# Two-layer hybrid decoder on one core: another order of copies, squares, splits and transposes where a layer begins

## The chip, the cores and the metric

The kernel runs on one core of one Trainium2 chip. The metric is the device time of one execution in microseconds, the median of several runs; lower is better. The core has five engines that work side by side, each through its own queue in order: PE (matrix products), ACT (ScalarE), DVE (VectorE), POOL (GpSimd) and SP, which here only issues DMAs. An engine waits at the head of its queue until what the instruction needs is there; nothing behind it can overtake.

## What is computed

Two layers act on x (256 rows, 2048 columns, float32). Cut to what matters here:

```python
for l in range(2):
    h = rms_norm(x, norm_pre[l])              # x * rsqrt(mean(x*x)) * g
    proj = h @ w_in[l]                        # q, k, v, gates, S5 and pool inputs
    att = nsa_mixer(...)                      # sparse attention
    ssm = s5_mixer(...)                       # state-space layer
    pool = pool_mixer(...)
    out = concat(att, ssm, pool) @ w_out[l]
    x = x + rms_norm(out, norm_post[l])
```

## The kernel before

**Products in three passes.** Each float32 operand is split into a high and a low part. ACT writes the high part (`split`, L311, a copy), DVE the low part (L317, the difference), and `mm3` (L387, L388, L389) adds high·high, high·low and low·high. So every block of weights needs one ACT and one DVE instruction before PE can use it. Weights come as a stream of pieces; a piece has two halves of 128x1024, which SP loads into five `raw` buffers in order (`load`, L285).

**Where a layer begins.** x is used transposed (`hT`, high and low). `turn(l, t, x, hT, c)` makes four of its 128x128 blocks: t is the row block (0 or 1), c a chunk of 512 columns (0 to 3). PE transposes (L411), ACT writes the high parts (L415), DVE the low ones (L421). The first product of a layer is `vs`: `vsel(n, t, c)` multiplies chunk (t, c) with half c of the four `vs` halves, 12 matmuls each, and sums over c in one PSUM bank per t. The normalisation is by the row, so the factor `rr` is multiplied in afterwards: the squares of x are summed (`square_sum`, ACT, L938; in the first layer some on DVE, L978), `rstd_of` takes the power of -0.5 on POOL (L397), `vsel_out(t)` scales the finished `vs` bank out of PSUM (L381 on ACT, L382 on DVE), and `row_factors` spreads `rr` along the columns (L433 on DVE, L434 on PE, L436).

**PSUM banks.** The tag `pp` has three banks. The two `vs` sums hold two, the first of the `u5` products (48 matmuls each; here U0, U1, U2) takes the third. U1 needs the bank that `vsel_out(0)` frees, U2 that of `vsel_out(1)`.

**Where a layer ends.** `wo` sums the output projection over 16 steps for each of four column chunks. For the last chunk (`mm_last(t, d)`, 12 matmuls for each t and d) the order is written by hand together with the start of the next layer: `ev_wo` squares the sum (ACT) and multiplies it with the norm weights (DVE, L1227), `rstd_of` gives the factor (DVE L395, then POOL L397), `update` adds the result to x (DVE, L1234, four chunks), and `turn` follows.

**What sets the order.** Inside `with tc.manual_schedule(engines=ORDERED)` each engine's queue has the order of the code. Outside, a scheduler places the instructions at build time; these may also be put among those written by hand. Of the S5 layer, `s5_chain` clears two matrices (`sa`, `sb`) in which only blocks are written later. The 128x2048 tiles of tag `m8` have four places: three hold `vs` halves, later `sa`, `sb` and the mixed outputs lie there. At the end of a layer the four mixed outputs fill them, so the next layer's second `vs` half can only be split when `mm_last(1, 0)` has read the first mixed output.

Of the kernel before, what the change touches and what calls it, by code (L numbers as in the profile page):

```python
# [138 lines left out]
def body(ctx, tc, a):  # L139
# [35 lines left out]
    X = {}  # L175
# [278 lines left out]
    def s5_chain(l):  # L454
# [8 lines left out]
        with after("pool"):  # L463
            G.memset(sa[:, 1024:], 0.0)
            G.memset(sb[:, :1280], 0.0)
# [476 lines left out]
    hT = new_hT()  # L942
# [8 lines left out]
    with tc.manual_schedule(engines=ORDERED):  # L951
        warm = st([128, 256], "r1", bufs=2)
        V.memset(warm, 0.0)
        load_x0(0, 0, 512)
        nc.sync.dma_start(cn[:, :160], a["cst"][:, :160])
        load_x0(0, 1, 512)
        load(0, (0,))
        load_x0(0, 2, 512)
        load_x0(0, 3, 512)
# [3 lines left out]
        load(1)  # L963
        nc.sync.dma_start(cn[:, 160:], a["cst"][:, 160:])
        nc.sync.dma_start(sm, a["sm"])
        load(2)
        wp = pp()
        for _ in range(5):
            T.matmul(wp[:, :256], lhsT=warm[:, :128], rhs=warm, start=True, stop=True)

        def both(t, c):
            low = turn(0, t, xt[t], hT, c)
            low()
# [9 lines left out]

        both(0, 0)
        both(0, 1)
        split(0, 0)
        both(0, 2)
        both(0, 3)
        sq_a(0, 0)
        vsel(0, 0, 0)  # L990
        both(1, 0)
        both(1, 1)
        vsel(0, 1, 0)
        split(0, 1)
        sq_a(0, 1)
        vsel(0, 0, 1)
        vsel(0, 1, 1)
        both(1, 2)
        split(1, 0)
        both(1, 3)  # L1000
        vsel(0, 0, 2)
        vsel(0, 1, 2)
        split(1, 1)
        sq_a(0, 2)
        sq_a(0, 3)
        vsel(0, 0, 3)
        vsel(0, 1, 3)
        sq_v(1, 0)
        sq_v(1, 1)
        sq_a(1, 2)  # L1010
        sq_a(1, 3)
        for t in range(2):
            X["norm"] = rstd_of(sqs[t], dst=X["rr"][:, t:t + 1]) and X["norm"]
# [3 lines left out]
    while n < nst:  # L1017
# [49 lines left out]
        elif kind == "vs":  # L1067
            X["gates"] = st([128, 2, 24], "gates")
            load(n + 4)
            with after("norm"), after("act"):  # L1070
                for h in range(2):
                    split(n + 2, h)
                for t in range(2):
                    vsel_out(t)
                row_factors()
# [118 lines left out]
        else:  # L1194
# [28 lines left out]
            def ev_wo(t, c):  # L1223
                p = X["op"][t]
                cs = slice(c * 512, (c + 1) * 512)
                square_sum(p, X["osq"][t], c)
                V.tensor_tensor(X["og"][t][:, cs], p, X["gpost"][:, cs], op=ALU.mult)  # L1227

# [21 lines left out]
            elif q == 0:  # L1250
# [8 lines left out]
                if l + 1 == NL:  # L1259
                    for t in range(2):  # L1260
                        for d in range(4):
                            mm_last(t, d)
                        ev_wo(t, 3)
                        update(t, rstd_of(X["osq"][t]))
                else:
# [4 lines left out]
                    def squares(t):  # L1270
                        for c_ in range(4):
                            square_sum(X["xt"][t][:, c_ * 512:(c_ + 1) * 512], sqs[t], c_)
                        rstd_of(sqs[t], dst=rr[:, t:t + 1])

                    with tc.manual_schedule(engines=ORDERED):
# [3 lines left out]
                        ev_wo(0, 3)  # L1279
# [123 lines left out]
```

## Time and profile before

| what | value |
|---|---|
| median of 3 runs | 884.55 us (883.99 to 885.16) |
| the profiled execution's own time | 880.77 us |
| its span, first to last instruction | 879.0 us |
| PE busy | 857.0 us of the span (97%) |
| DVE, ACT, POOL busy | 649.9, 487.9, 34.9 us |
| mean granted PE clock | 0.993 of full speed |

The profile is of one execution. PE is almost never idle, so the question is where in the span its 22 us without work lie: the page's tenths and the table by stretches show the first 30 us, some of 440 to 470 us (the border between the layers) and the last 9 us. Times in the rows count from the start of the span. "Idle before" and the name behind the arrow say how long an engine stood before an instruction and what ended that.

### The profile page before, as it was taken

What the parts mean: (1) busy time and instruction counts of PE and PEld (TensorE: products, weight loads), DVE (VectorE), ACT (ScalarE), POOL (GpSimd) and SP (SyncE); (2) the same over time, 40 slices, a digit from 0 to 9 for tenths busy, and PEclk for the clock granted to TensorE, in tenths of its full rate; (3) what the DMA queues carried; (4) which work ended last, traced back from release to release, by engine and by line L of the source; (5) the groups of instructions that cost most, each with busy time, mean ns of one, the idle gap of its engine ahead of it and who ended that gap; (6) DMA issues with size and microseconds to landing.
All of it is one profiled execution on the core that took longest, in us unless ns stands there. A gap on an engine that the chain in (4) does not pass through costs nothing.

```text
span 879.0 us, 17460 instructions
## 1 busy us (share of the span) xinstructions
PE 857.0 (97%) x6858; PEld 793.4 (90%) x6858; DVE 649.9 (74%) x1365; ACT 487.9 (56%) x961; POOL 34.9 (4%) x64
## 2 busy tenths in 40 slices
PE   7899999999999999999998999999999999999996
PEld 5898899999999999888898988999999999998884
DVE  4997889796887877557588676979778788765553
ACT  5755557584767743446375525475647666434440
POOL 0240000000000000000001300000000000000000
PEclk9999999999999999999998999999999999999998
DMA  8777656443445755557355577664444457456642
GB/s 296 243 211 264 244 194 203 139 146 121 147 141 164 250 196 170 192 191 265 142 195 191 167 290 262 194 200 120 146 129 160 128 184 264 149 187 191 191 145 97
DMA packets 46259, 165.04 MB, mean 188 GB/s; under 512 B 5536, under 2 KB 5792, under 8 KB 45152
## 3 DMA queue, kind: packets, MB, share of 16 engines
q1 hardware_dynamic: 43632, 154.22, 53.4%
q0 software_dynamic: 2544, 9.70, 3.1%
q8 instruction: 54, 0.88, 0.4%
q14 instruction: 29, 0.24, 0.1%
HBM read 158.66 MB, written 4.19 MB: 185 GB/s over the span
## 4 chain that ended last, share of the span: by engine, by line
PE 93%; DVE 2%; issue 2%; ACT 1%; DMA 1%; POOL 0%; DVEq 0%; POOLq 0%; ACTq 0%
PE pp L387 24%; PE pp L389 23%; PE pp L388 23%; PE acc L389 3%; PE acc L387 3%; PE acc L388 3%; PE acc L1113 2%; PE sc L592 2%; PE tr L749 1%; PE acc L597 1%; DVE hT L421 1%; PE tr L568 1%; PE acc L620 1%; DMA raw<-in_w 1%; PE sc L389 1%
## 5 line engine op out<-in xcount | busy, mean ns | idle before, releaser
L311 ACT ACTIVATE whi<-raw 128x1024 fp32r<-128x1024 f32 (+2 forms) x238 | 248.7, 1048 | 241.0 <-PE pp L388 103.0
L387 PE MATMUL pp<-hT,whi 128*128 128x256 f32 x1280 | 367.8, 287 | 2.2 <-DVE rs L403 2.0
L317 DVE TENSOR_TENSOR wlo<-raw,whi 128x1024 fp32r<-128x1024 f32 (+2 forms) x238 | 287.0, 1208 | 109.4 <-ACT whi L311 107.3
L388 PE MATMUL pp<-hT,whi 128*128 128x256 f32 x1280 | 365.1, 285 | 0.0
L389 PE MATMUL pp<-hT,wlo 128*128 128x256 f32 x1280 | 364.9, 285 | 0.0
L387 PEld LDWEIGHTS pp<-hT,whi 128*128 128x128 f32 x1280 | 246.0, 192 | 8.3 <-issue 4.9
L389 PEld LDWEIGHTS pp<-hT,wlo 128*128 128x128 f32 x1280 | 246.1, 192 | 3.2 <-issue 1.2
L388 PEld LDWEIGHTS pp<-hT,whi 128*128 128x128 f32 x1280 | 246.2, 192 | 1.4 <-issue 0.6
L388 PE MATMUL acc<-wlo,m 128*128 128x512 f32 x112 | 44.0, 393 | 0.0
L387 PE MATMUL acc<-whi,m 128*128 128x512 f32 x112 | 43.7, 390 | 0.0
L387 PE MATMUL pp<-whi,m 128*128 128x512 f32 x112 | 43.6, 390 | 0.0
L388 PE MATMUL pp<-wlo,m 128*128 128x512 f32 x112 | 43.6, 389 | 0.0
L389 PE MATMUL pp<-whi,m 128*128 128x512 f32 x112 | 43.6, 389 | 0.0
L389 PE MATMUL acc<-whi,m 128*128 128x512 f32 x112 | 43.6, 389 | 0.0
L512 ACT ACTIVATE m<-m 64x256 f32<-64x256 f32 x64 | 26.4, 413 | 11.8 <-DVE m L510 11.1
L378 ACT ACTIVATE a<-tr 128x256 fp32r<-128x256 f32 (+1 forms) x32 | 15.6, 488 | 24.9 <-PE tr L749 24.5
L734 ACT ACTIVATE P<-sc,sv 128x128 f32<-128x128 f32 (+1 forms) x64 | 26.1, 414 | 5.9 <-DVE scv L795 3.5
L742 ACT ACTIVATE P<-P,sv 128x128 f32<-128x128 f32 (+1 forms) x64 | 25.5, 448 | 2.0 <-DVE sv L740 1.0
L389 PEld LDWEIGHTS pp<-whi,m 128*128 128x128 f32 x112 | 21.0, 188 | 4.4
L389 PEld LDWEIGHTS acc<-whi,m 128*128 128x128 f32 x112 | 21.0, 188 | 4.4
L388 PEld LDWEIGHTS acc<-wlo,m 128*128 128x128 f32 x112 | 21.0, 188 | 4.3
L388 PEld LDWEIGHTS pp<-wlo,m 128*128 128x128 f32 x112 | 21.0, 188 | 4.3
(300 smaller groups left out, 1355.9 us busy)
## 6 DMA issues: line engine op xcount, KB each, us to landing
raw<-in_w SPq DMA_DIRECT2D x272, 512.0 KB, 3.6
raw<-in_w SPq DMA_DIRECT2D x8, 420.0 KB, 4.6
a<-in_gpost POOLq DMA_DIRECT2D x2, 1024.0 KB, 4.9
a<-in_x POOLq DMA_DIRECT2D x2, 1024.0 KB, 6.6
xs<-a SPq DMA_DIRECT2D x2, 1024.0 KB, 3.8
a<-xs POOLq DMA_DIRECT2D x2, 1024.0 KB, 7.5
out_dram<-a SPq DMA_DIRECT2D x8, 256.0 KB, 2.5
raw<-in_w SPq DMA_DIRECT2D x4, 280.0 KB, 3.1
```

The source lines that it names most:

```text
L311: A.activation(hi[:, :w], raw[:, :w], AF.Copy)
L317: V.tensor_tensor(lo[:, :w], raw[:, :w], hi[:, :w].bitcast(F32), op=ALU.subtract)
L378: A.activation(hi, src, AF.Copy)
L387: T.matmul(out, lhsT=lh, rhs=rh, start=start, stop=False, **kw)
L388: T.matmul(out, lhsT=lh, rhs=rl, start=False, stop=False, **kw)
L389: T.matmul(out, lhsT=ll, rhs=rh, start=False, stop=stop, **kw)
L421: X["norm"] = V.scalar_tensor_tensor(hT[1][:, k, ts], p[:, j * 128:(j + 1) * 128], C["gT"][:, l * 16 + k:l * 16 + k + 1], hT[0][:, k, ts]. ...
L512: A.activation(dst[64 * g:64 * g + 64, :, k0:k0 + 4, 16 * g:16 * g + 16], x[64 * g:64 * g + 64], AF.Copy)
L592: T.matmul(xv[:, i, m_, :], lhsT=IN[:, i, m_, :], rhs=u4[:, i, t, :], start=True, stop=True)
L734: A.activation(P[:, b], pv[:, b], AF.Exp, scale=-1.0, bias=sv[:, 0, b:b + 1], accum_out=sv[:, 1, b:b + 1])
L742: A.activation(P[:, b], P[:, b], AF.Copy, scale=sv[:, 2, b:b + 1])
L1113: T.matmul(hm[32 * j:32 * j + 32, :256], lhsT=blk[:, lk, :], rhs=raw[:, j * 256:j * 256 + 256], start=lk < 4, stop=lk >= 28, tile_position ...
```

## The change

The order of the instructions where each layer begins is written anew; two matrices are cleared on another engine; one warm-up matmul is added.

- At the first layer's start SP loads the first `vs` half before x, and the transposes, copies, splits, products and squares are interleaved in another way. The squares of the first row block stand together on ACT ahead of the others' end, `rstd_of` for that block follows at once, and `vsel_out(0)` and the splits of U0 move into the part written by hand.
- At the border of the layers `ev_wo` runs `rstd_of` ahead of the multiplication with the norm weights; the first row block's squares come before its transposes, the second's between its transposes; both splits of a piece come earlier; `vsel_out(0)` and the splits of U0 are written by hand ahead of the last two `vs` products.
- In the last layer `ev_wo` gets the same order of `rstd_of` and multiplication.
- `sa` and `sb` are cleared by ACT (a copy with scale 0) instead of two POOL memsets.

```diff
-        with after("pool"):
-            G.memset(sa[:, 1024:], 0.0)
-            G.memset(sb[:, :1280], 0.0)
+        for z in (sa[:, 1024:], sb[:, :1280]):
+            A.activation(z, bc(ident[:, 0:1], [128, z.shape[1]]), AF.Copy, scale=0.0)
...
-        load_x0(0, 0, 512)
+        load(0, (0,))
         nc.sync.dma_start(cn[:, :160], a["cst"][:, :160])
-        load_x0(0, 1, 512)
-        load(0, (0,))
-        load_x0(0, 2, 512)
-        load_x0(0, 3, 512)
+        for c in range(4):
+            load_x0(0, c, 512)
         load_x0(1, 0, 1024)
         load(0, (1,))
         load_x0(1, 1, 1024)
         load(1)
+        load(2, (0,))
         nc.sync.dma_start(cn[:, 160:], a["cst"][:, 160:])
         nc.sync.dma_start(sm, a["sm"])
-        load(2)
+        load(2, (1,))
         wp = pp()
-        for _ in range(5):
+        for _ in range(6):
...
+        split(0, 0)
         both(0, 0)
         both(0, 1)
-        split(0, 0)
         both(0, 2)
+        both(1, 0)
+        vsel(0, 0, 0)
+        split(0, 1)
         both(0, 3)
-        sq_a(0, 0)
-        vsel(0, 0, 0)
-        both(1, 0)
         both(1, 1)
         vsel(0, 1, 0)
-        split(0, 1)
-        sq_a(0, 1)
         vsel(0, 0, 1)
+        split(1, 0)
+        both(1, 2)
         vsel(0, 1, 1)
-        both(1, 2)
-        split(1, 0)
+        vsel(0, 0, 2)
+        split(1, 1)
         both(1, 3)
-        vsel(0, 0, 2)
         vsel(0, 1, 2)
-        split(1, 1)
-        sq_a(0, 2)
-        sq_a(0, 3)
         vsel(0, 0, 3)
-        vsel(0, 1, 3)
+        split(2, 0)
+        for c in range(4):
+            sq_a(0, c)
+        rstd_of(sqs[0], dst=X["rr"][:, 0:1])
         sq_v(1, 0)
         sq_v(1, 1)
+        split(2, 1)
         sq_a(1, 2)
         sq_a(1, 3)
-        for t in range(2):
-            X["norm"] = rstd_of(sqs[t], dst=X["rr"][:, t:t + 1]) and X["norm"]
+        vsel_out(0)
+        vsel(0, 1, 3)
+        rstd_of(sqs[1], dst=X["rr"][:, 1:2])
...
-            def ev_wo(t, c):
+            def ev_wo(t, c, first=None):
                 p = X["op"][t]
                 cs = slice(c * 512, (c + 1) * 512)
                 square_sum(p, X["osq"][t], c)
+                r = None if first is None else rstd_of(X["osq"][t], first)
                 V.tensor_tensor(X["og"][t][:, cs], p, X["gpost"][:, cs], op=ALU.mult)
+                return r
...
-                        ev_wo(t, 3)
-                        update(t, rstd_of(X["osq"][t]))
+                        update(t, ev_wo(t, 3, rstd_first(X["osq"][t])))
...
                         first = rstd_first(X["osq"][0])
-                        ev_wo(0, 3)
+                        r = ev_wo(0, 3, first)
                         mm_last(1, 0)
                         mm_last(1, 1)
                         hT = new_hT()
-                        r = rstd_of(X["osq"][0], first)
-                        split(m, 0)
                         update(0, r, False)
                         keep(0)
+                        split(m, 0)
+                        split(m, 1)
+                        for c_ in range(4):
+                            sq_a(0, c_)
                         for c_ in range(4):
                             turn(l + 1, 0, X["xt"][0], hT, c_)()
                         X["hT"] = hT
-                        split(m, 1)
                         mm_last(1, 2)
                         split(m + 1, 0)
+                        split(m + 1, 1)
                         mm_last(1, 3)
                         first = rstd_first(X["osq"][1])
-                        ev_wo(1, 3)
-                        r = rstd_of(X["osq"][1], first)
-                        split(m + 1, 1)
+                        r = ev_wo(1, 3, first)
                         update(1, r, False)
                         keep(1)
...
+                            if c_ == 1:
+                                rstd_of(sqs[0], dst=rr[:, 0:1])
+                            if c_ == 2:
+                                split(m + 2, 0)
+                            sq_a(1, c_)
+                        vsel_out(0)
+                        split(m + 2, 1)
                         vsel(m, 1, 2)
                         vsel(m, 1, 3)
-                        squares(1)
+                        rstd_of(sqs[1], dst=rr[:, 1:2])
```

**Place 1: ACT at the first layer's start.** Before, the queue begins as below. `tr`, `sc`, `acc` are the banks of the transposes of chunks 0, 1, 2 and, with `sc` again, 3; `a_1` and `a_2` are the two row blocks of x; `m_18`, `m_27`, `m_30` are `vs` halves 0, 1, 2.

```order
L415 ACTIVATE hT_84<-tr_120,cn 128x128 x4
L415 ACTIVATE hT_84<-sc_133,cn 128x128 x4
L311 ACTIVATE m_18_146<-raw_96 128x1024
L415 ACTIVATE hT_84<-acc_149,cn 128x128 x4
L415 ACTIVATE hT_84<-sc_162,cn 128x128 x4
L938 ACTIVATE mr_175,sq_86<-a_1_82 128x512
L415 ACTIVATE hT_84<-tr_192,cn 128x128 x4
L415 ACTIVATE hT_84<-sc_205,cn 128x128 x4
L311 ACTIVATE m_27_230<-raw_101 128x1024
L938 ACTIVATE mr_233,sq_86<-a_1_82 128x512
L1156 ACTIVATE hb_3848<-sm 128x8
L415 ACTIVATE hT_84<-acc_259,cn 128x128 x4
```

Now the same queue, with halves 0, 1, 2 in `m_16`, `m_24`, `m_27`:

```order
L311 ACTIVATE m_16_121<-raw_93 128x1024
L415 ACTIVATE hT_84<-tr_124,cn 128x128 x4
L415 ACTIVATE hT_84<-sc_137,cn 128x128 x4
L415 ACTIVATE hT_84<-acc_150,cn 128x128 x4
L415 ACTIVATE hT_84<-tr_163,cn 128x128 x4
L311 ACTIVATE m_24_191<-raw_101 128x1024
L415 ACTIVATE hT_84<-sc_194,cn 128x128 x4
L415 ACTIVATE hT_84<-sc_207,cn 128x128 x4
L311 ACTIVATE m_27_244<-raw_104 128x1024
L464 ACTIVATE m_66_500<-cn 128x1024
L464 ACTIVATE m_67_501<-cn 128x1280
L415 ACTIVATE hT_84<-acc_247,cn 128x128 x4
```

The split of half 0 moved to the front, chunk (1, 0) ahead of (0, 3), half 2 ahead of chunk (1, 2); the squares moved behind these rows, and the two clearings (L464) stand ahead of chunk (1, 2).

**Place 2: DVE at the border of the layers.** Before, from the low parts of the first row block's last chunk to the low parts of the second's first chunk. `acc_5119` is the bank of `mm_last(1, ...)`, `a_660` the second row block of x.

```order
L421 SCALAR_TENSOR_TENSOR hT_5236<-sc_5286,cn,hT_5235 128x128 x4
L317 TENSOR_TENSOR m_771_5299<-raw_5122,m_771_5299 128x1024
L317 TENSOR_TENSOR m_772_5314<-raw_5128,m_772_5314 128x1024
L402 TENSOR_REDUCE rs_5329<-sq_4659 128x1
L403 TENSOR_SCALAR rs_5329<-rs_5329 128x1
L1227 TENSOR_TENSOR a_655_4654<-acc_5119,a_656_4655 128x512
L395 SCALAR_TENSOR_TENSOR rs_5329<-sq_4659,rs_5329 128x1
L317 TENSOR_TENSOR wlo_5338<-raw_5130,whi_5337 128x1024
L1234 SCALAR_TENSOR_TENSOR a_660_4662<-a_655_4654,rs_5329,a_660_4662 128x512 x4
L421 SCALAR_TENSOR_TENSOR hT_5236<-tr_5373,cn,hT_5235 128x128 x4
```

Now the same stretch, where the bank is `acc_5120`:

```order
L421 SCALAR_TENSOR_TENSOR hT_5239<-sc_5298,cn,hT_5238 128x128 x4
L317 TENSOR_TENSOR m_776_5323<-raw_5129,m_776_5323 128x1024
L484 TENSOR_TENSOR m_816_5596<-rot 128x512
L544 TENSOR_TENSOR m_816_5596<-spv,cn 128x256
L317 TENSOR_TENSOR wlo_5327<-raw_5131,whi_5326 128x1024
L402 TENSOR_REDUCE rs_5342<-sq_4660 128x1
L403 TENSOR_SCALAR rs_5342<-rs_5342 128x1
L395 SCALAR_TENSOR_TENSOR rs_5342<-sq_4660,rs_5342 128x1
L1223 TENSOR_TENSOR a_655_4655<-acc_5120,a_656_4656 128x512
L1231 SCALAR_TENSOR_TENSOR a_660_4663<-a_655_4655,rs_5342,a_660_4663 128x512 x4
L421 SCALAR_TENSOR_TENSOR hT_5239<-tr_5382,cn,hT_5238 128x128 x4
```

The last step of the row factor (L395) moved ahead of the multiplication, the split of the fourth `vs` half ahead of both, and two S5 instructions (L484, L544) came in between; half 1 is split earlier, ahead of these rows.

**Place 3: ACT behind the second row block's last transposes.** Before, from these transposes' copy to the scaling of the first `vs` bank (L381). `sq_5152` and `sq_5153` take the squares of the two row blocks.

```order
L415 ACTIVATE hT_5235<-sc_5448,cn 128x128 x4
L938 ACTIVATE mr_5473,sq_5152<-a_659_4660 128x512
L311 ACTIVATE whi_5533<-raw_5140 128x1024
L311 ACTIVATE whi_5537<-raw_5142 128x1024
L311 ACTIVATE whi_5566<-raw_5524 128x1024
L938 ACTIVATE mr_5475,sq_5152<-a_659_4660 128x512
L311 ACTIVATE whi_5601<-raw_5526 128x1024
L311 ACTIVATE whi_5638<-raw_5529 128x1024
L938 ACTIVATE mr_5510,sq_5153<-a_660_4662 128x512
L311 ACTIVATE whi_5668<-raw_5531 128x1024
L381 ACTIVATE a_777_5346<-pp_5347,rr_5154 128x256
```

(Of the eight squares three stand here; the others lie between the same rows.) Now, from the clearing of `sa` on:

```order
L464 ACTIVATE m_815_5595<-cn 128x1024
L937 ACTIVATE mr_5345,sq_4660<-acc_5120 128x512
L464 ACTIVATE m_816_5596<-cn 128x1280
L415 ACTIVATE hT_5238<-tr_5382,cn 128x128 x4
L937 ACTIVATE mr_5407,sq_5154<-a_660_4663 128x512
L415 ACTIVATE hT_5238<-sc_5409,cn 128x128 x4
L415 ACTIVATE hT_5238<-acc_5441,cn 128x128 x4
L311 ACTIVATE whi_5466<-raw_5141 128x1024
L415 ACTIVATE hT_5238<-sc_5472,cn 128x128 x4
L937 ACTIVATE mr_5497,sq_5154<-a_660_4663 128x512
L381 ACTIVATE a_781_5355<-pp_5356,rr_5155 128x256
```

The scaling of the first bank moved from behind six splits and eight squares to the place right behind the last transposes' copy and its square.

## Rows read from the trace of the kernel before

**Rows 1.** The page, busy time of each engine.

```profile
PE 857.0 (97%) x6858; PEld 793.4 (90%) x6858; DVE 649.9 (74%) x1365; ACT 487.9 (56%) x961; POOL 34.9 (4%) x64
```

**Rows 2.** Stretches: length, busy time and instructions of each engine, PE clock, DMA share, GB/s.

```profile
50.00:60.00 10.00, 10.00 (x86) 10.00 (x85) 10.00 (x23) 5.41 (x8) 3.95 (x7) 1.00 0.61 197
...
466.00:468.00 2.00, 2.00 (x11) 2.00 (x11) 2.00 (x2) 0.10 (x1) 2.00 (x3) 0.50 0.72 203
```

**Rows 3.** Timeline of PE at the start: start, length, instruction.

```profile
24.68 0.39 PE L388 MATMUL pp<-m,hT 128*128 128x256 f32 x1 [0.96 <-DVE m L317]
...
36.30 0.36 PE L387 MATMUL pp<-hT,whi 128*128 128x256 f32 x1
```

**Rows 4.** SP's timeline, and DMA issues of 3.3 to 3.8 us with median time to landing.

```profile
3.07 1.21 SPq L949 DMA_DIRECT2D a<-in_x  x2
...
a<-in_x SPq DMA_DIRECT2D x1, 512.0 KB, 7.2
```

**Rows 5.** Timeline of ACT in the first 31 us.

```profile
8.62 1.11 ACT L311 ACTIVATE m<-raw 128x1024 fp32r<-128x1024 f32 x1
9.57 1.19 ACT L415 ACTIVATE hT<-acc,cn 128x128 fp32r<-128x128 f32 x4
10.56 1.23 ACT L415 ACTIVATE hT<-sc,cn 128x128 fp32r<-128x128 f32 x4
...
29.35 0.63 ACT L938 ACTIVATE mr<-a 128x512 f32<-128x512 f32 x1
...
30.10 0.63 ACT L938 ACTIVATE mr<-a 128x512 f32<-128x512 f32 x1
```

**Rows 6.** Costliest groups of the page, the S5 copy: busy and mean ns.

```profile
L512 ACT ACTIVATE m<-m 64x256 f32<-64x256 f32 x64 | 26.4, 413 | 11.8 <-DVE m L510 11.1
```

**Rows 7.** Timelines of ACT, DVE, POOL and PE at the border, 429 to 446 us.

```profile
434.04 1.14 ACT L415 ACTIVATE hT<-tr,cn 128x128 fp32r<-128x128 f32 x4 [4.19 <-PE tr L411]
...
439.37 2.35 DVE L317 TENSOR_TENSOR m<-raw,m 128x1024 fp32r<-128x1024 f32 x2
...
442.48 0.15 DVE L395 SCALAR_TENSOR_TENSOR rs<-sq,rs 128x1 f32<-128x1 f32 x1
442.55 1.22 DVE L317 TENSOR_TENSOR wlo<-raw,whi 128x1024 fp32r<-128x1024 f32 x1
444.21 2.74 DVE L1234 SCALAR_TENSOR_TENSOR a<-a,rs,a 128x512 f32<-128x512 f32 x4 [0.44 <-POOL rs L397]
...
442.71 1.46 POOL L397 TENSOR_TENSOR rs<-rs,mhalf 128x1 f32<-128x1 f32 x1 [12.36 <-DVE rs L395]
...
430.46 0.39 PE L389 MATMUL acc<-hT,m 128*128 128x512 f32 x1
...
445.02 0.66 PE L411 MATMUL tr<-cn,a 128*128 128x128 f32 x4 [1.38 <-DVE a L1234]
```

**Rows 8.** Timelines of PE and DVE at the border, 460 to 471 us.

```profile
461.80 0.49 PE L434 MATMUL sc<-r,r 128*128 128x128 f32 x2 [0.43 <-DVE r L433]
464.31 0.58 PE L387 MATMUL pp<-hT,whi 128*128 128x256 f32 x1 [2.02 <-DVE rs L403]
...
470.60 0.28 PE L387 MATMUL pp<-hT,whi 128*128 128x256 f32 x1
...
463.78 0.47 DVE L382 SCALAR_TENSOR_TENSOR a<-pp,rr,a 128x256 fp32r<-128x256 f32 x1
464.50 0.68 DVE L485 TENSOR_TENSOR m<-rot 128x512 f32<-128x512 f32 x1
465.11 0.42 DVE L545 TENSOR_TENSOR m<-spv,cn 128x256 f32<-128x256 f32 x1
```

**Rows 9.** Timelines of DVE and POOL behind PE's last matmul.

```profile
871.03 0.69 DVE L1227 TENSOR_TENSOR a<-acc,a 128x512 f32<-128x512 f32 x1 [6.69 <-ACT mr L938]
...
872.45 2.74 DVE L1234 SCALAR_TENSOR_TENSOR a<-a,rs,a 128x512 f32<-128x512 f32 x4 [0.66 <-POOL rs L397]
...
871.87 0.55 POOL L397 TENSOR_TENSOR rs<-rs,mhalf 128x1 f32<-128x1 f32 x1 [10.31 <-DVE rs L395]
```

More of the change, by code (lines that the diff above doesn't have):

```diff
@@ L963, in body @@
         load(1)
+        load(2, (0,))
         nc.sync.dma_start(cn[:, 160:], a["cst"][:, 160:])
         nc.sync.dma_start(sm, a["sm"])
-        load(2)
+        load(2, (1,))
         wp = pp()
-        for _ in range(5):
+        for _ in range(6):
             T.matmul(wp[:, :256], lhsT=warm[:, :128], rhs=warm, start=True, stop=True)
         def both(t, c):
-            low = turn(0, t, xt[t], hT, c)
-            low()
+            turn(0, t, xt[t], hT, c)()
         def sq_v(t, c):
@@ L1070, in body @@
             with after("norm"), after("act"):
[L1071 to L1074, printed above, removed]
+                vsel_out(1)
                 row_factors()
@@ L1268, in body, with sq_a @@
                     rr = st([128, 2], "rr", bufs=2)
[L1270 to L1273, printed above, removed]
+                    def sq_a(t, c_):
+                        square_sum(X["xt"][t][:, c_ * 512:(c_ + 1) * 512], sqs[t], c_)
                     with tc.manual_schedule(engines=ORDERED):
@@ L1289, in body @@
                         X["hT"] = hT
-                        split(m, 1)
                         mm_last(1, 2)
                         split(m + 1, 0)
+                        split(m + 1, 1)
                         mm_last(1, 3)
                         first = rstd_first(X["osq"][1])
-                        ev_wo(1, 3)
-                        r = rstd_of(X["osq"][1], first)
-                        split(m + 1, 1)
+                        r = ev_wo(1, 3, first)
                         update(1, r, False)
                         keep(1)
+                        X["rr"] = rr
                         vsel(m, 0, 0)
@@ L1307, in body @@
                                 vsel(m, 1, c_ - 2)
-                        squares(0)
+                            if c_ == 1:
[5 more added lines that the diff above has]
+                        split(m + 2, 1)
                         vsel(m, 1, 2)
                         vsel(m, 1, 3)
-                        squares(1)
+                        rstd_of(sqs[1], dst=rr[:, 1:2])
                         X["rr"] = rr
```

## Prediction

> **What bounds the kernel now.** I read the page first: PE is busy for 857.0 of 879.0 us, DVE for 649.9, ACT for 487.9 [rows 1]. An order can give back only the 22 us in which PE has no work, and time in which its clock is low. The table by stretches says where these are not: from 50 to 60 us PE is full at clock 1.00, and so is DVE [rows 2]. They are at both ends and at the border between the layers, so I went through the timelines of these places.
>
> At the start PE stands again and again until 24.68, where a low-part product ends the last stall (it waited 0.96 for DVE). From there PE runs on through 48 `vs` matmuls and the 48 of U0 to the first matmul of U1 at 36.30 [rows 3]; 96 matmuls at the 0.116 to 0.12 us of a full stretch (86 in 10 us) are 11.5 us [rows 2]. So what the new start is worth is read from when U1 begins.
>
> At the border PE stands twice. The transposes of the second row block, t(1,0), start at 445.02 after 1.38 without work, waiting for `update` [rows 7]. U1 starts at 464.31 after 0.43 ahead of `row_factors` and 2.02 for a `pp` bank; the bank came free with L382 (463.78 plus 0.47) [rows 8]. The second stand costs more than its 2.45 us: the granted clock is 0.50 (the 1.2 GHz level) behind it [rows 2], and the 28 matmuls from 464.31 to 470.60 took 6.3 us where 0.12 each would give 3.4 [rows 8].
>
> At the end DVE multiplies (871.03), then does L395 (871.64), POOL the power (871.87, 0.55 long), and `update` begins at 872.45 [rows 9].
>
> **The change, part by part.** *Start.* I worked the new ACT queue through by the distance from one start to the next: a split 0.95 (8.62 to 9.57), a chunk's copies 1.0 (9.57 to 10.56), a square 0.75 (29.35 to 30.10) [rows 5]. Loading half a weight first delays the first transposes, but the bytes ahead of chunk (1,0) are the same in both orders: issued at about 3.5, the second of the two in that row, it lands 7.2 later, at 10.7 [rows 4]. From its transposes on ACT has no free time, by these prices: copies of (1,0) start at 11.4; with those of (0,3) and (1,1) and the split of half 1 it is 15.35; split of half 2, 16.3; the two clearings, taken at a split's rate (0.95 and, for 1280 columns, 1.19), 18.4; copies (1,2), half 3, a small copy (estimate 0.2), copies (1,3), first half of U0, four squares, second half of U0: 26.5. Then the two splits of U1, a square, a small copy, a split of U2 and a square: 31.0, and L381 (as L382, 0.47): 31.5. L382 on DVE ends at 32.0 and frees U1's bank [rows 8]. PE is ready by then: the last U0 product can begin when its split is there at 26.5 plus DVE's 1.2, with 24 matmuls behind it, 2.9 us. The same reckoning on the old queue ends at 35.6 where the row has 36.30, so I add 0.7: U1 at 32.8. **The start gives 3.5 us.** One bound: ACT clears as slowly as its S5 copy, 0.413 for 256 columns [rows 6], 1.6 ns a column against 0.93, so 3.7 instead of 2.1, and 1.9 is left. The other: no hand-over is lost, 4.2. The cover behind it: the later banks are freed at about 36, before U2 (38.5) asks. POOL no longer clears; it stands idle 96% of the time [rows 1], so taking that off it gives nothing by itself.
>
> *Border.* The early split of `vs` half 1 needs a place that `mm_last(1,0)` frees; that product's last matmul ends at 430.46 + 0.39 = 430.85. Then split (0.95) and four squares (3.0) stand ahead of the first copy: 434.85 instead of 434.04, 0.81 late [rows 5, 7]. DVE's low parts follow it, so its next split starts at 440.18, not 439.37. Behind it come the split (half of 2.35, 1.18), L484 (0.61, from 464.50 to 465.11), L544 (as L545, 0.42) and the second split (1.18): 443.57; then L402, L403 at L395's 0.15 each, and L395 at 443.87 [rows 7, 8]. The square of the bank on ACT has sa's clearing (0.95) ahead, but before it had ended by about 442.2 (L395 at 442.48 less 0.3) [rows 7], so DVE's row comes later by 1.3 and binds. POOL starts 0.23 behind L395, as at 442.48 and 442.71, at 444.10.
>
> How long the power takes is open. At this place it took 1.46, beside a split whose two inputs lie in SBUF (442.55 to 443.77), and `update` began 0.04 behind it at 444.21 [rows 7]; at the end, with no DVE work beside it, 0.55 [rows 9]. Now the multiplication L1223 runs beside it, which reads one input from PSUM. I take 0.55, since the slow row is one with both inputs in SBUF; the other end is to be held until the multiplication (0.69 long, from about 444.0) is over, 0.35 more. The Trainium skill, "SBUF — State Buffer", section "SBUF: two separate sides", has a rule here: DVE and GpSimd share a pair of ports as an exclusive lock, which a DVE instruction with two SBUF inputs holds for its whole length against a GpSimd one that reads SBUF. By that rule this multiplication holds nothing and the power takes 0.55; the trace's 1.46 beside the split agrees, and no row yet shows the power beside L1223.
>
> So `update` starts at 444.69 and t(1,0), 0.81 behind as before, at 445.50: half a microsecond **later** than now, with a stand of about 1.8 where it was 1.38 [rows 7]. What follows gains: `vsel_out(0)` now stands right behind the last transposes on ACT, at some 454, so the bank is free 6 us or more ahead of U1. PE then runs on: 445.50 plus the 16.35 from 445.02 to U0's end (461.80 less 0.43) is 461.85; `row_factors` 0.49; 28 matmuls of U1 at 0.12, 3.36: 465.70 where the row has 470.60 [rows 7, 8]. **The border gives 4.9 us**: 2.45 of stand and 2.9 of clock, less 0.48. Bounds: 2.0 where the clock falls again at the longer stand, 6.5 where PE doesn't wait ahead of t(1,0) at all.
>
> *End.* L395 starts at 871.03 where the multiplication did, the power runs beside the latter, `update` starts 0.6 earlier: 871.85. Held until the multiplication ends it is 0.2 [rows 9]. **The end gives 0.6.**
>
> The sum is 3.5 + 4.9 + 0.6 = 9.0. The profiled execution took 880.77, 3.8 less than the median of 884.55 (its span plus 1.77); 871.8 for such an execution, and **875.5** for the median.
>
> **The rivals.**
>
> *The clock is lost again at the border.* For it: the stand of 1.8 ahead of t(1,0) is nearer than 1.38 was to the 2.45 behind which the clock fell. Against: it is still shorter, and the products behind the 1.38 ran at the full rate (the 16.35 us to U0's end) [rows 7, 8]. Price 2.9: 878.4.
>
> *The earlier U1 at the start is given back.* DVE is full from 50 to 60 us [rows 2]; if its backlog sets PE's pace there, U1 three microseconds earlier only means a longer wait for low parts later, or the clock falls early in the stand before chunk (1,0) and costs as much (28 matmuls slowed, 2.9, as at the border). Against: PE has no idle time in that stretch. Without the start's term: 879.0.
>
> *Nothing much happens at either place:* start given back and clock lost again leave 9.0 − 3.5 − 2.9 = 2.6 (881.9), and a power held at border and end takes 0.75 of it: 882.7, about at the 0.2% (1.8 us) below which a measurement of this kernel can't tell a change.
>
> *Slower: clearing on ACT costs several times a split.* No row shows a copy from one broadcast column. Call k the time for both matrices, 2.1 in my sum. At the start all of k beyond 2.1 stands ahead of chunk (1,2) and comes back one to one; at the border sa's share (44%) stands ahead of the square on which `update` hangs, free up to 1.3 and one to one beyond, and then the clock (2.9) goes too. The kernel is slower by over 1.8 when 1.44 (k − 2.1) − 1.3 + 2.9 exceeds 10.8: k about 8.5, or 3.7 ns a column, where the rows have 0.93 and 1.6 [rows 5, 6]. At k = 10 it gives 13.0 − 9.0 = 4.0 more than now: 888.5. Against: nothing in the rows is near this.
>
> **How the numbers follow.** My forecast has 0.60, the clock lost again 0.13, the start given back 0.15, both together 0.06, the dear clearing 0.06. The first three are faster by more than 0.2%, 0.88; of "both together" I put 0.01 more there and 0.05 on no change; slower is 0.06. The sums of the terms' bounds are 4.2 + 6.5 + 0.6 = 11.3 and 1.9 + 2.0 + 0.2 = 4.1, so 873.2 to 880.4; that takes in the first three cases, and 12 in 100 lie above it.
>
> **What would show it.** In the changed profile U1 (the second `u5` product) should begin at about 33 us. At the border no row of PE should name a wait for a `pp` bank, no stretch between 460 and 470 should have clock 0.50, t(1,0) should still wait for `update` for 1.4 to 1.9, and the first copy there should stand at 434.85 less the start's gain. The rows of L464 on ACT should be about 1.0 and 1.3 long, the power beside L1223 0.55, and the last `update` should begin 0.85 after the square's end rather than 1.45. The forecast is wrong if U1 is early and a later wait of PE for DVE grows by as much, if t(1,0) is over 2 us late and the clock falls there, or if L464 takes several microseconds.

## The result: 1.2% faster here, 0.8 to 0.9% in two later measurements

The changed kernel took 873.34 us (median of 4, 872.62 to 876.45) beside 884.42 us for the kernel before: ratio 0.9881, 95% interval 0.9856 to 0.9905, 11.1 us less where 9.0 were forecast (875.5, range 873.2 to 880.4), just inside the range's lower end. Two later measurements, each beside new runs of the kernel before (median 881.9), gave 0.9915 (0.9895 to 0.9935) and 0.9912 (0.9890 to 0.9935), 7.5 and 7.8 us. The intervals overlap; 7 to 11 us is what the runs support. Differences of the experiments below are worked out as one less the ratio, times 882.

The two profiled executions must not simply be subtracted. The one of before took 880.77 us, 3.7 less than its median here; the one of the changed kernel took 876.45, the slowest of its four. Single executions of either kernel differ by up to 6 us, and the profiles below show a good part of why.

The page of the changed kernel, busy time of each engine (compare [rows 1]):

```profile
PE 854.4 (98%) x6860; PEld 791.6 (91%) x6860; DVE 647.7 (74%) x1365; ACT 491.8 (56%) x965; POOL 29.9 (3%) x60
```

Stretches of the changed kernel: length, busy time and instructions of PE, PEld, DVE, ACT, POOL, PE's clock, DMA share, GB/s (compare [rows 2, 8]):

```profile
50.00:60.00 10.00, 10.00 (x86) 10.00 (x85) 10.00 (x25) 5.00 (x7) 4.35 (x8) 1.00 0.64 191
82.00:84.00 2.00, 1.55 (x8) 1.35 (x9) 1.23 (x1) 1.95 (x8) 0.00 (x0) 0.79 0.92 377
84.00:86.00 2.00, 2.00 (x11) 2.00 (x11) 0.97 (x1) 1.49 (x2) 0.00 (x0) 0.50 0.73 231
460.00:470.00 10.00, 10.00 (x86) 10.00 (x85) 8.13 (x13) 5.60 (x10) 1.81 (x5) 1.00 0.93 349
```

The border is now full and at clock 1.00 from 460 to 470 us. But there is a stretch at 0.50 (the 1.2 GHz level) at 84 us that the profile of before doesn't have. PE's timeline of the changed kernel shows what is ahead of it (start, length, instruction, in brackets the idle time and what ended it; compare [rows 3]):

```profile
31.94 0.39 PE L387 MATMUL pp<-hT,whi 128*128 128x256 f32 x1 [1.00 <-DVE rs L402]
...
73.59 0.39 PE L387 MATMUL pp<-hT,whi 128*128 128x256 f32 x1 [1.68 <-ACT whi L311]
74.85 0.39 PE L389 MATMUL pp<-hT,wlo 128*128 128x256 f32 x1 [0.19 <-DVE wlo L317]
79.99 0.55 PE L567 MATMUL tr<-cn,m 128*128 128x128 f32 x3 [0.55 <-ACT m L511]
81.11 0.43 PE L572 MATMUL sc<-m,m 128*32 128x128 f32 x8 [0.57 <-ACT m L511]
82.19 0.38 PE L387 MATMUL pp<-hT,whi 128*128 128x256 f32 x1 [0.66 <-ACT whi L311]
82.95 0.94 PE L567 MATMUL tr<-cn,m 128*128 128x128 f32 x4 [0.26 <-ACT m L576]
...
100.68 0.33 PE L567 MATMUL tr<-cn,m 128*128 128x128 f32 x1 [0.56 <-ACT m L511]
```

U1 starts 4.36 us earlier than before, but between 73 and 102 us PE now stands 4.5 us for splits and for the S5 chain, where before it stood 0.59 (once, at 101.32, for a weight piece). So in this execution the start's gain is given back here. What makes the S5 chain late is read on ACT and DVE of the changed kernel, 41 to 47 us:

```profile
43.88 0.42 ACT L470 ACTIVATE a<-a 128x256 f32<-128x256 f32 x1 [3.56 <-DMA a<-in_cb]
...
45.26 1.06 ACT L311 ACTIVATE whi<-raw 128x1024 fp32r<-128x1024 f32 x1
...
46.35 1.23 DVE L317 TENSOR_TENSOR wlo<-raw,whi 128x1024 fp32r<-128x1024 f32 x1 [4.47 <-ACT whi L311]
```

ACT stands at L470 for a load of S5 constants (`cb`), with a weight split queued behind it; DVE stands for that split, and the S5 parameters are queued behind DVE's half of it. The load is issued on POOL behind the second row block's power (POOL's timeline of the changed kernel):

```profile
25.51 0.94 POOL L397 TENSOR_TENSOR rr<-rs,mhalf 128x1 f32<-128x1 f32 x1 [24.25 <-DVE rs L395]
33.52 0.69 POOL L397 TENSOR_TENSOR rr<-rs,mhalf 128x1 f32<-128x1 f32 x1 [7.08 <-DVE rs L395]
34.17 0.70 POOL L1031 DMA_DIRECT2D pw<-in_pw  x1
34.88 0.54 POOL L467 DMA_DIRECT2D a<-in_cb  x1
```

In the kernel before it went out later, since the two clearings stood ahead of it on POOL (POOL's timeline of before):

```profile
37.27 0.54 POOL L468 DMA_DIRECT2D a<-in_cb  x1
```

It goes out 2.4 us earlier now, but took 9.0 us to land where before it took 6.9, so it lands at 43.9 where it landed at 44.2. What made it slower is not shown.

The border of the changed kernel, on ACT, DVE, POOL and PE (compare [rows 7]):

```profile
432.55 1.06 ACT L311 ACTIVATE m<-raw 128x1024 fp32r<-128x1024 f32 x1 [1.02 <-PE acc L389]
...
436.40 1.12 ACT L415 ACTIVATE hT<-tr,cn 128x128 fp32r<-128x128 f32 x4
...
445.36 0.16 DVE L395 SCALAR_TENSOR_TENSOR rs<-sq,rs 128x1 f32<-128x1 f32 x1
445.44 0.68 DVE L1223 TENSOR_TENSOR a<-acc,a 128x512 f32<-128x512 f32 x1
446.18 2.74 DVE L1231 SCALAR_TENSOR_TENSOR a<-a,rs,a 128x512 f32<-128x512 f32 x4
...
445.60 0.55 POOL L397 TENSOR_TENSOR rs<-rs,mhalf 128x1 f32<-128x1 f32 x1 [14.18 <-DVE rs L395]
...
446.99 0.66 PE L411 MATMUL tr<-cn,a 128*128 128x128 f32 x4 [1.68 <-DVE a L1231]
```

And its end, ACT, DVE and POOL (compare [rows 9]; this view of DVE ends within the last update, so its row has three of the four chunks):

```profile
866.63 0.60 ACT L937 ACTIVATE mr<-acc 128x512 f32<-128x512 f32 x1 [10.19 <-PE acc L389]
...
867.35 0.16 DVE L395 SCALAR_TENSOR_TENSOR rs<-sq,rs 128x1 f32<-128x1 f32 x1 [7.29 <-ACT mr L937]
867.43 0.69 DVE L1223 TENSOR_TENSOR a<-acc,a 128x512 f32<-128x512 f32 x1
868.17 2.08 DVE L1231 SCALAR_TENSOR_TENSOR a<-a,rs,a 128x512 f32<-128x512 f32 x3
...
867.59 0.55 POOL L397 TENSOR_TENSOR rs<-rs,mhalf 128x1 f32<-128x1 f32 x1 [10.31 <-DVE rs L395]
```

To follow where time comes and goes through all runs, one reading is used from here on, the **shift**: the start of a PE matmul in a run's profile less the start of the same matmul in the profile of before (the median over a stretch of 6 us). It stays constant from 140 us to the border, so four numbers tell an execution. Where the scheduler placed PE's instructions in another order than before (80 to 150 us in all runs with the new start, 500 to 545 us in two runs below and from 500 us on in a third), it also holds what that order costs or saves. Worked out from the PE timelines:

```
run                        45-66  140-428     475     650 us
changed kernel             -4.34    +1.67   -3.77   -3.68
start alone                -4.24    +0.82   -0.43   -0.72
border and end alone       +0.15    +0.70   -5.68   -4.28
changed, clearing on POOL  -2.27    +3.80   -2.58   -2.54
changed, second run        -2.54    -0.62   -6.05   -6.02
changed, third run         -2.97    +3.05   -2.39   -2.40
cb early                   -4.46    -2.90   -8.33   -8.34
cb early, late split       -3.70    -3.57   -9.52   -7.96
the same, second run       -4.06    -1.22   -7.19   -7.26
start alone, cb early      -4.05    -2.53   -5.17   -7.08
```

In the changed kernel the start gives 4.3, 6.0 are lost between 66 and 140 us, the border gives 5.4. Of the 6.0, 3.9 are stands (4.5 less 0.6). The lowered clock makes some 1.7 (2 us at 0.79, 2 at 0.50, and 2 at 0.85 from 86 to 88 us); 0.4 are not accounted for.

### The profile page after: what moved, and what is told of

It reads as the page before. It is cut to its first block, busy times and chain, and to the rows that moved or that the text cites. A ratio compares the mean times of both kernels' runs of the same rounds, so it can differ in the third digit from the quotient of the medians.

```text
span 874.6 us, 17467 instructions
## 1 busy us (share of the span) xinstructions
PE 854.4 (98%) x6860; PEld 791.6 (91%) x6860; DVE 647.7 (74%) x1365; ACT 491.8 (56%) x965; POOL 29.9 (3%) x60
## 4 chain that ended last, share of the span: by engine, by line
PE 83%; DVE 5%; DMA 4%; ACT 3%; issue 3%; POOL 0%; SPq 0%; DVEq 0%; POOLq 0%; ACTq 0%
PE pp L387 21%; PE pp L389 21%; PE pp L388 21%; PE acc L388 3%; PE acc L389 3%; PE acc L387 3%; DMA raw<-in_w 2%; PE sc L591 2%; DVE wlo L317 1%; PE tr L748 1%; PE acc L1108 1%; DMA a<-in_cb 1%; PE acc L596 1%; PE tr L567 1%; ACT whi L311 1%
## 5 line engine op out<-in xcount | busy, mean ns | idle before, releaser
L511 ACT ACTIVATE m<-m 64x256 f32<-64x256 f32 x64 | 26.4, 412 | 8.7 <-DVE m L509 8.0
```

Source lines behind the costliest of these rows:

```text
L511: A.activation(dst[64 * g:64 * g + 64, :, k0:k0 + 4, 16 * g:16 * g + 16], x[64 * g:64 * g + 64], AF.Copy)
```

## The experiments

Two theories: **kept**, by which what the start gains reaches the end, as the prediction has it; and **given back**, by which the weights and the S5 chain of 62 to 83 us come no earlier than before. For the second the suspects are the `cb` load and DVE's own backlog.

**The kernel before once more**, without an edit.

> The kernel before once more, for a second profile: the profiled execution shown lies 3.7 us under the median of the timed ones (880.77 against 884.42), while the changed kernel's profiled one lies 3.1 us over its median. Theory A: executions differ by one stretch of half clock of some 3 us price, at another place than 463 to 470 us; a profile at about 884 then shows a second stretch at clock 0.50 or new waits of PE, and a profile at about 881 none. Theory B: the difference lies outside the work of PE (before the first or behind the last instruction); then the span less the time's rest changes and PE's rows stand where they stood. Timed ratio 1.000.

880.85 us, ratio 1.0003 (0.9988 to 1.0018). Its profile has the span of the first one, but the clock fell at another place too. Stretches of this run:

```profile
26.00:28.00 2.00, 2.00 (x12) 2.00 (x11) 2.00 (x7) 2.00 (x3) 0.00 (x0) 0.50 0.76 221
28.00:30.00 2.00, 2.00 (x16) 2.00 (x16) 2.00 (x4) 1.97 (x7) 0.00 (x0) 0.85 0.59 223
...
466.00:468.00 2.00, 2.00 (x12) 2.00 (x11) 1.89 (x4) 0.47 (x1) 2.00 (x3) 0.50 0.73 234
468.00:470.00 2.00, 2.00 (x15) 2.00 (x15) 1.45 (x2) 0.00 (x0) 2.00 (x5) 0.77 0.95 256
```

Behind the start's stands PE ran at 0.50, which it did not in the first profile, and at the border the slow stretch was shorter. So executions of one kernel do differ by where the clock falls and for how long, as theory A has it. But theory A expected no second slow stretch in a profile at 881, and the slowest executions (884) were not profiled. The mean granted clock of every timed execution is on record: of the 33 of the kernel before measured here, the six at 0.997 took 879.4 to 880.7 us and the five at 0.990 or less 881.5 to 884.2, while one at 0.996 took 883.3. The clock is a good part of the spread, and not all of it.

**The start alone.** The new lines of the first layer's start in the kernel before; in the second layer the splits and `vsel_out(0)` stay where they were.

```diff
+                if l == 0:
+                    vsel_out(1)
+                else:
+                    for h in range(2):
+                        split(n + 2, h)
+                    for t in range(2):
+                        vsel_out(t)
```

> Only the first layer's start is new (loads, the sixth warm-up matmul, the interleaving, first bank's scaling and U0's splits by hand); border, end and clearing as before. Theory A (given back): U1 starts at about 32, 4.4 us earlier than before, but the weight pieces that land between 62 and 83 us come at most 1 us earlier, since their five places come free by a chain of landing, split and next load; PE waits there 1.5 to 3 us, so the kernel is 1.4 to 2.5 us faster (ratio 0.997 to 0.9985), and less where the clock falls behind these waits. Theory B (the prediction's): nothing is given back, 3.5 to 4.4 us faster, ratio 0.995 to 0.996.

879.71 us, ratio 0.9981 (0.9964 to 0.9998): 1.7 us of the 4.4. U1 starts at 31.80. PE's timeline of this run shows the changed kernel's stands, without the longest (1.68 at 73.59):

```profile
78.18 0.55 PE L568 MATMUL tr<-cn,m 128*128 128x128 f32 x3 [0.51 <-ACT m L512]
79.30 0.43 PE L573 MATMUL sc<-m,m 128*32 128x128 f32 x8 [0.57 <-ACT m L512]
80.38 0.56 PE L387 MATMUL pp<-hT,whi 128*128 128x256 f32 x1 [0.66 <-ACT whi L311]
```

The clock is 0.50 from 82 to 86 us behind them. Given back, theory A. In this profile the shift goes from -4.24 to +0.82: 1.7 of the 5.1 are stands (2.3 less 0.6), and the rest is the clock (0.61 from 80 to 82 us, 0.50 to 86, 0.69 to 88). The stands alone would leave some 2.5: the two executions of this run with a mean clock of 0.996 or more took 876.9 and 877.4 us, the six of the kernel before at 0.997 took 879.4 to 880.7.

**The border and the end alone**, with the start and the POOL memsets of before.

> Only the border between the layers and the order at the end are new; the start and the clearing (POOL) as before. Theory A: the border gives 5 to 5.6 us and the end 0.6, about 6 us, ratio 0.9925 to 0.994; no row of PE names a wait for a pp bank at the border, and clock 1.00 from 460 to 470. Theory B: most of the measured 11 us comes from here, 8 or more, ratio under 0.991, because executions of the kernel before lose the clock a second time behind the border's waits.

875.71 us, ratio 0.9935 (0.9918 to 0.9952): 5.7 us, theory A. No wait for a `pp` bank and clock 1.00 at the border; the shift goes from +0.70 to -5.68 there. It then loses 1.4 at the second layer's S5 chain and weights (518 to 526 us).

**The changed kernel with the clearing back on POOL.**

```diff
-        for z in (sa[:, 1024:], sb[:, :1280]):
-            A.activation(z, bc(ident[:, 0:1], [128, z.shape[1]]), AF.Copy, scale=0.0)
+        with after("pool"):
+            G.memset(sa[:, 1024:], 0.0)
+            G.memset(sb[:, :1280], 0.0)
```

> The changed kernel with the two clearings back on POOL. Theory A: clearing costs nothing on either engine where it stands: ACT's start is not the pace from chunk (1,2) on, so U1 starts within 0.3 us of 31.94, and the time is within 0.2% of the changed kernel's, 873. Theory B (the prediction's working): ACT is the binding queue, and 2.1 us less on it let U1 start 1 to 2 us earlier (30 to 31), time 871 to 872. Theory C: the memsets on POOL hold DVE's instructions where they share a port; U1 later by 1 us or more, or t(1,0) later.

873.62 us, ratio 0.9913 (0.9885 to 0.9942), the same as the changed kernel's 0.9915 as far as these intervals tell: theory A in time. U1 starts at 33.78 here, not at 31.94, but its clock was 0.50 from 12 to 14 us, behind the stand for x, which costs this much in the changed kernel too (next run). At the border the stand ahead of t(1,0) is 0.7 instead of 1.7, since L484 and L544, which write into the tile of `sb`, no longer come ahead of the row factor on DVE. The shift gains 6.4 at this border, as in the border alone, and 5.4 in all three profiles of the changed kernel, so there the clearing on ACT costs about 1 us.

**The changed kernel again**, twice, without an edit, each time beside new runs of the kernel before.

> The changed kernel once more, beside the kernel before and the other runs of this call. The parts alone gave 1.8 (start) and 5.8 us (border and end), 7.6 together, where the whole gave 11.1 against another chip's runs of before. Theory A (parts add up): ratio 0.990 to 0.992, 7 to 9 us. Theory B (they work on each other, or the clearing gives the rest): 0.987 to 0.988, 10.5 us or more.

> The changed kernel a third time. Theory A: 7 to 8 us faster than before (0.991 to 0.992) as in the second run, the 11 of the first being of other executions; its profile shows a stretch of half clock either behind the start's stand at 10 to 16 us or behind the stands at 73 to 83. Theory B: 10 us or more.

874.54 us, ratio 0.9915 (0.9895 to 0.9935), and 874.91, 0.9912 (0.9890 to 0.9935). Theory A both times: the 1.7 of the start and the 5.7 of border and end add up to 7.4, the whole measured 7.5 and 7.8. The profile of the second run loses the clock early and keeps it at 84 us (stretches):

```profile
12.00:14.00 2.00, 2.00 (x12) 2.00 (x11) 1.20 (x5) 1.71 (x4) 0.00 (x0) 0.50 1.03 422
...
84.00:86.00 2.00, 2.00 (x23) 1.67 (x22) 1.23 (x1) 1.03 (x3) 0.00 (x0) 1.00 0.97 381
```

U1 started at 33.74 there, 1.8 later, and the stands behind it shrank to 2.5 us. The third run lost it at both places and took 877.73 in that execution; the fastest of its six took 871.69.

**cb early.** In the changed kernel the two loads on POOL go behind the first row block's power instead of the second's.

```diff
         rstd_of(sqs[0], dst=X["rr"][:, 0:1])
+        p_rr0 = X["pool"]
...
         rstd_of(sqs[1], dst=X["rr"][:, 1:2])
+        X["pool"] = p_rr0
```

> The changed kernel with the two loads on POOL's queue (pw and cb) issued behind the first row block's power instead of the second's. Theory A: what gives the start's gain back is the cb load: it lands at 43.9 whatever the start does, ACT stands 3.6 us for it at 43.88 with a split behind, DVE 4.5 us behind that, and the S5 instructions are as late as before when PE asks for them at 73 to 83. With cb landing by 36, DVE has no stand over 1.5 us between 36 and 48, PE stands less than 1 us in all from 70 to 90 (4.2 now), and the time falls by 2 to 4 us against the changed kernel. Theory B: DVE's own work sets these times (it is full from 50 to 65 us): DVE's row of the split at 49.9 moves by under 1 us, PE's stands stay, time the same within 1 us.

873.47 us, ratio 0.9907 (0.9887 to 0.9927). The load is issued at 26.98, and ACT's timeline of this run has

```profile
32.38 0.42 ACT L470 ACTIVATE a<-a 128x256 f32<-128x256 f32 x1 [0.60 <-DMA a<-in_cb]
...
74.23 1.74 ACT L511 ACTIVATE m<-m 64x256 f32<-64x256 f32 x4 [4.66 <-DVE m L509]
```

ACT reaches L511, which the S5 transposes wait for, at 74.23 instead of 78.20 (77.98 before the change): the `cb` load did set the S5 chain's time, and DVE's backlog didn't. PE's timeline of this run, all stands from 40 to 140 us:

```profile
78.25 0.39 PE L387 MATMUL pp<-hT,whi 128*128 128x256 f32 x1 [0.46 <-ACT whi L311]
79.01 0.66 PE L567 MATMUL tr<-cn,m 128*128 128x128 f32 x4 [0.26 <-ACT m L576]
...
96.30 0.33 PE L567 MATMUL tr<-cn,m 128*128 128x128 f32 x1 [1.43 <-ACT m L511]
```

From 70 to 90 us 0.7 is left, as theory A had it, but a new stand of 1.4 stands at 96: the second turn of the S5 chain waits for the weights again (its ACT row L511 has a split ahead that stood 5.7 for a `raw` piece). 2.15 less the 0.59 of before is the 1.56 by which the shift falls from -4.46 to -2.90. By the ratios the step is 0.7 us against the changed kernel, less than the 2 to 4 expected and within the spread; the mechanism is shown by the rows, its whole worth is not kept.

**cb early in the start alone.**

> Only the new start (border, end and clearing as before), with the two loads moved on POOL's queue as in the run with cb early. Theory A: the start's whole 4.4 us are kept, ratio 0.9945 to 0.996 where the start alone had 0.998. Theory B: 0.997 to 0.9985 as the start alone.

876.82 us, ratio 0.9935 (0.9911 to 0.9958) where the start alone had 0.9981: 5.7 us, 4.0 more than the start alone, theory A a little exceeded. Two things in its profile, which is that of the fastest of its six executions (873.75), weigh against reading too much into that. Its border is the old one, with the same stands of 0.43 and 2.02 (U1 at 461.77), yet the clock there stayed at 1.00, and the shift gains 2.6 us that the change did not make. And between 516 and 540 us it gains another 1.9 (0.3 in the start alone): the scheduler placed PE's instructions in another order there, and three stands of 0.7 us in all that the kernel before has at 528 to 531 us are gone. So the load's share of the 4.0 is smaller, and how large is not shown.

**cb early and the late split**, run twice. At the border the split of the fourth `vs` half goes behind the second update.

```diff
-                        split(m + 1, 1)
                         mm_last(1, 3)
...
                         update(1, r, False)
+                        split(m + 1, 1)
                         keep(1)
```

> As the run before, and at the border the split of the fourth vs half stands behind the second update on DVE instead of ahead of the row factor. Theory A (DVE's row sets the transposes of the second row block): they start 1.1 us earlier against the copies ahead of them, PE's stand for update falls from 1.7 to about 0.6, 1 us faster than the run before. Theory B: that stand is hidden later (U1's bank or the weights), no difference.

> The kernel with the two loads early on POOL's queue and the fourth half's split behind the second update once more, beside the changed kernel on the same chip (the next run), to say which is faster. Theory A: 2 to 3 us faster than the changed kernel. Theory B: the same within the spread of the executions.

871.80 us, ratio 0.9886 (0.9867 to 0.9905), and 872.65, 0.9894 (0.9875 to 0.9913), beside 874.54 and 874.91 of the changed kernel measured with them: 2.6 and 1.6 us faster by the ratios, though the intervals overlap. It has the lowest median of all versions. The list of PE's waits of the first of these runs has, for t(1,0) (us in total, times, longest):

```profile
PE tr L411 <- DVE a L1233: 0.4, 1, 0.4
```

instead of 1.7, so DVE's row did set the second update, as theory A says. But a stand of 0.48 for the late split itself comes behind it (at 443.62), and the shift gains 5.95 and 5.97 at this border where cb early alone gained 5.43: of the 1.3, half a microsecond is left.

**One pair of instructions at the border.** In the kernel before, `vsel_out(0)` alone goes ahead of the second row block's squares.

```diff
                         squares(0)
+                        X["rr"] = rr
+                        vsel_out(0)
                         vsel(m, 1, 2)
```

> The kernel before with one instruction pair moved: at the border the scaling of the first vs bank stands behind the first row block's squares, ahead of the second's, so some 3 us earlier on ACT. Start, end, clearing and all else as before. Theory A (bank and clock): PE's stand of 2.0 us ahead of U1 goes, the clock doesn't fall behind it, and this alone gives 4.5 to 5.3 us, ratio 0.994 to 0.995, nearly all that the border gives. Theory B (only the stand): 2.0 us, the clock falls all the same behind the other stands of the border (1.4 and 0.4), ratio 0.9975 to 0.998.

879.43 us, ratio 0.9974 (0.9962 to 0.9986): 2.3 us, which is theory B's size but not its cause. ACT and PE of this run:

```profile
463.05 1.06 ACT L311 ACTIVATE whi<-raw 128x1024 fp32r<-128x1024 f32 x1 [1.21 <-PE pp L388]
464.01 0.46 ACT L381 ACTIVATE a<-pp,rr 128x256 fp32r<-128x256 f32 x1
...
465.82 0.39 PE L387 MATMUL pp<-hT,whi 128*128 128x256 f32 x1 [1.76 <-DVE a L382]
```

The scaling was moved past the second row block's squares, but a split still stands ahead of it, and this split waits for a place that PE's own products free. PE's stand for the bank is 0.26 shorter, where some 3 us were expected of the scaling. By the shift the profile gains 1.2 at the border (from +1.76 to +0.54), where the stretch of low clock is also shorter, and 2.2 more by 540 us, where the scheduler placed PE's instructions in another order and the three stands at 528 to 531 us are gone, as in cb early in the start alone. So the run doesn't test what it was made for; its rows show that the splits ahead of the scaling, not those squares, kept the bank. The change takes the scaling ahead of both.

**The clearing alone**, on ACT, in the kernel before.

> The kernel before with the two clearings on ACT alone. Theory A: no difference, within 0.2%. Theory B: ACT's 2.1 us stand on the path at the start (it frees U1's bank later, U1 at 38 instead of 36.3), up to 2 us slower, ratio 1.002.

884.17 us, ratio 1.0032 (1.0018 to 1.0046): 2.8 us slower. U1 comes at 37.48, 1.2 later and near the 38 of theory B, but that is the smaller part: the shift is +1.21 at 45 to 66 us and +4.47 from 140. On POOL the powers were held twice (POOL and DVE of this run):

```profile
33.52 1.53 POOL L397 TENSOR_TENSOR rr<-rs,mhalf 128x1 f32<-128x1 f32 x1 [32.26 <-DVE rs L402]
35.52 1.59 POOL L397 TENSOR_TENSOR rr<-rs,mhalf 128x1 f32<-128x1 f32 x1 [0.47 <-DVE rs L395]
...
33.42 1.22 DVE L317 TENSOR_TENSOR wlo<-raw,whi 128x1024 fp32r<-128x1024 f32 x1
...
35.47 1.23 DVE L317 TENSOR_TENSOR wlo<-raw,whi 128x1024 fp32r<-128x1024 f32 x1
```

ACT's 2.1 us of clearing delay the squares, the powers then meet the splits on DVE, and further on PE stands 1.57 and 0.86 for `raw` pieces and 0.7 for a split. How the small delay becomes 3.3 us between 66 and 140 was not taken apart; the scheduler also placed other instructions differently there.

## Why the prediction came out as it did

**The start's own sum was right, and its correction wrong.** The walk along ACT's queue gave 32.1 for U1; the 0.7 added from the old order made it 32.8. It was 31.94. Two errors cancel in it: ACT was 0.7 ahead of the walk, and on DVE a split kept L382 waiting for as long (ACT and DVE of the changed kernel):

```profile
30.28 0.45 ACT L381 ACTIVATE a<-pp,rr 128x256 fp32r<-128x256 f32 x1
...
30.28 1.22 DVE L317 TENSOR_TENSOR wlo<-raw,whi 128x1024 fp32r<-128x1024 f32 x1
31.41 0.48 DVE L382 SCALAR_TENSOR_TENSOR a<-pp,rr,a 128x256 fp32r<-128x256 f32 x1
```

The clearings took 2.11 from start to start (2.14 in the sum), L381 stood at 30.28 (31.0), L382 ended at 31.9 (32.0).

**The step that failed is the cover behind the start.** "The later banks are freed at about 36, before U2 asks" was true and not enough. It looked at who waits for banks, not at what else stands on ACT's queue: L470 waits for the `cb` load, which hangs on the second row block's power on POOL. That power came only 0.5 earlier (33.52 and 34.06), and the load landed at 43.9 instead of 44.2, so a split, DVE and the S5 chain came no earlier while PE came 4.4 earlier. The rival "given back" (0.15) named this outcome, with two causes. DVE's backlog was not the cause: cb early moves the S5 chain by 4 us with DVE as full as before. The other, the clock lost early in the stand before chunk (1,0), did occur, in three of the nine profiles with the new start; in the changed kernel's second run U1 came 1.8 later with it. The prediction's own sign against itself came too: U1 is 4.4 early and PE's later stands grew by 3.9, for splits and copies on ACT rather than for DVE. The start's term was worth 1.7 us by time, not 3.5, because what it gained, 4.4, met waits that hadn't moved, and in five of the nine profiles a lower clock behind them.

**The border was forecast well.** 5.4 us by the shift in the profile and 5.7 with the end by time, where 4.9 and 0.6 were summed. In its steps: the first copy came 0.66 late against `mm_last(1,0)` (436.40 and 432.55, less 434.04 and 430.85 of [rows 7]; 0.81 forecast), t(1,0) 0.3 late (the shift goes from 1.67 to 1.97; 0.48 forecast) with a stand of 1.68 (1.8 forecast), and U1 had no wait and no low clock in any of the eight profiles with the new border. The rival of the clock lost again there did not occur. That the size fits is in part chance: the 2.9 for the clock was read from a profile whose slow stretch at the border was about twice as long as in the four others of the old border that had one. The upper bound of 6.5 comes out of its rows as 6.7 (2.45 + 2.9 + 1.38).

**The power took 0.55**, as chosen. Beside L1223, with one input in PSUM, it took 0.55; beside L975, whose two inputs lie in SBUF, 0.94 at the start; beside splits 1.53 and 1.59 in the run with the clearing alone. All four agree with the rule of the Trainium skill, "SBUF — State Buffer", section "SBUF: two separate sides", that a DVE instruction with two SBUF inputs which has started first holds up a GpSimd one that reads SBUF. A power that started first was not held: in the kernel before, one at 31.88 took 0.55 though a split ran beside it from 31.93.

**The end** gave 0.6: `update` began 1.54 behind the start of the last square (868.17 and 866.63), before 2.14 (872.45 in [rows 9]), and L395 stands where the multiplication did. The square of before, on ACT:

```profile
870.31 0.60 ACT L938 ACTIVATE mr<-acc 128x512 f32<-128x512 f32 x1 [10.19 <-PE acc L389]
```

**The clearing** costs on ACT what a split's rate says. As a part of this change it costs about 1 us at the border by the shift, and nothing that the times can tell. Alone in the old order it costs 2.8 us, which the prediction's rival of a dear clearing had not in mind: its price is not its length but what it pushes.

**The total was right partly by luck.** With the start's 1.7 in place of 3.5 and 5.7 in place of 5.5 for the rest, the sum is 7.4, what the later runs gave (7.5 and 7.8). The first measurement's 11.1 came with four executions of before at 884 to 885, the upper end of the 879 to 885 seen later; why they were all slow stays open. And of the changed kernel's four, three had a mean granted clock of 0.998 (872.6 to 873.5 us), as had only three of its later twelve (871.7 to 874.6); five of those, at 0.992 or 0.993, took 876.3 to 877.7.

## What to carry to other kernels

When a stretch is made earlier, follow every queue through the next thing that does not move with it: here a load issued on a quiet engine behind a wait, whose consumer stood at the head of a busy queue with a weight split behind it. A wait for a bank is set by what is queued ahead of the instruction that frees it; moving it past work that isn't waiting (four squares) brings almost nothing (0.26 us here) while a waiting split stays ahead. And where single executions differ by several us, read the shift of matmuls place by place, not the difference of two spans.

## What the hardware showed that was not expected

The clock does not fall each time behind the same stand. Of nine profiles with the new start, three were at 0.50 from 12 to 14 us, behind the stand for x's second row block (1.3 to 2.4 us long there, 1.4 to 1.9 in the six that kept the clock), and five near 84 us, two of them at both places. Near 84 us it fell behind stands of 1.1 to 3.9 us in all and was kept behind 0.7 to 2.1, so their sum does not decide it. At the old border, behind stands of 0.43 and of 1.8 to 2.0, it fell in five of six profiles and stayed at 1.00 in one. A forecast that books such a loss as certain, as this one did with 2.9 us at the border, books what holds for most executions only, and here the price was that of the longest such stretch of the five.
